# A two-layer hybrid decoder trunk on one core: GpSimd's tables and weight sums go to VectorE, the squared relu goes to ScalarE

## The chip, the core and the metric

The kernel runs on one core of a Trainium2 chip. The metric is the time of one execution on the device in microseconds (us); less is better. The engines are named as in the profile: PE is TensorE's matmul stream (PEld its weight loads), DVE is VectorE, ACT is ScalarE, POOL is GpSimd, and SP is SyncE, whose queue issues all the DMAs of this kernel. Each engine works through its own queue of instructions in order.

## What is computed

Two layers over a sequence of 1,024 positions and 1,024 channels, in float32. The reference, cut down:

```python
for l in range(2):
    h = rms_norm(x, mix_norm_g[l])
    # one projection: stick-breaking q/k/v, sliding-window q/k/v, two gates
    sb_q, sb_k, sb_v, sw_q, sw_k, sw_v, gate_logits = split(h @ w_in[l])
    y_sb = stick_breaking_attention(sb_q, sb_k, sb_v) @ w_branch_sb[l]
    q = apply_rope(rms_norm(sw_q, q_norm_g[l]), cos, sin)
    k = apply_rope(rms_norm(sw_k, k_norm_g[l]), cos, sin)
    y_swa = sliding_window_sink_attention(q, k, sw_v, sinks[l]) @ w_branch_swa[l]
    g = sigmoid(gate_logits).reshape(B, S, 2, D)
    x = x + (g[:, :, 0] * y_sb + g[:, :, 1] * y_swa) @ w_out[l]
    h2 = rms_norm(x, mlp_norm_g[l])
    x = x + square(relu(h2 @ w_up[l])) @ w_down[l]      # 1024 -> 4096 -> 1024
```

## The kernel before

Every product is made in three matmuls: each operand is split into a high part in the type fp32r (a cast on ScalarE) and the rest (a subtraction on VectorE), and the function `three` multiplies high by high, high by rest and rest by high. So a 128-row block of an operand costs one ScalarE instruction and one VectorE instruction (`split`, lines 1266 and 1269; `fetch`, lines 332 and 335, for other weights) before TensorE can use it.

A layer runs in four stages: norm and gates, sliding-window attention beside stick-breaking attention, merge and output projection, and the MLP. The MLP's two products are each made by a scheme with seven block products in the place of eight (numbered "1" to "7"), whose operands are sums and differences of quarters of the matrices.

- **First product** (`up_phase`). The weights of one of 16 pairs come in two DMAs of 512 KB, `ra` and `rb`, into two buffers named `raw`. Products 1 and 2 use the halves of `ra` as they are. Products 3 to 7 use sums: `operands` makes four of them from `a11`, `a12` (`ra`) and `a21`, `a22` (`rb`), in place or into a `stage` buffer, and then splits them into buffers `wh` and `wl`. The four sums are GpSimd's (line 1283, the "G" branch of `two`). TensorE does the products of a pair in the order 1, 2, 6, 5, 3, 4, 7, and each product is 12 matmuls of 512 columns. `pair` adds the seven results into four blocks on VectorE (line 1583), squares their positive part (`relu2`, line 1542), makes the sums for the second product (line 1280) and writes all of it to a scratch tensor `u_scr`. A buffer of `rb` comes free when product 7's operand has been split.
- **Second product** (`down_phase`). SP loads 512 KB pieces of `u_scr` and of `w_down` into buffers named `dr`, and they are split into tiles named `operand`.
- **Sliding-window attention.** `consts` scales a table `gt` and the sinks `snk`; `tables` multiplies `gt` with the rotation of one block of 128 positions into a table `tab`, eight per layer, and saves it. Those three are GpSimd's too (lines 510, 512, 547). An iteration's VectorE chain reads `tab` (lines 626 and 628), adds (633), splits (662, 644), and TensorE transposes the result (lines 668 and 650).

The order of the instructions on each engine is set when the program is built: a planner (`Plan`) gives every step an engine and a cost, such as

```python
yield "G", gps(n)        # n * .00195 + .4 us on GpSimd
yield "D", dve(n)        # n * .00104 + .068 us on VectorE
yield "A", act(n)        # n * .00083 + .095 us on ScalarE
```

and writes the instructions out in the order in which its own clock comes to them. That order is then fixed, so an instruction whose input is late holds up all that stands behind it on its engine.

Of the kernel before, what the change touches and what calls it, by code (L numbers as in the profile page):

```python
# [12 lines left out]
AF = mybir.ActivationFunctionType  # L13
ALU = mybir.AluOpType
AX = mybir.AxisListType

P = 128
T = 1024
D = 1024
HD = 64  # L20
# [178 lines left out]
def tile_hybrid_trunk(ctx: ExitStack, tc: tile.TileContext, x, g_mix, g_mlp, g_rope, sinks, rope,  # L199
                      w_swa, w_qk, w_v, w_gate, w_br, w_out, w_up, w_down, out):  # L200
    nc = tc.nc
# [50 lines left out]
    def act(n):  # L252
        return n * .00083 + .095

    def dve(n):
        return n * .00104 + .068

    def gps(n):
        return n * .00195 + .4
# [7 lines left out]
    def moved(n):  # L267

        return "M", n / 380e3, 0
# [24 lines left out]
    def stage_tile():  # L294
        return gp.tile([P, 512], F32, tag="stage", name="stage", bufs=4)
# [184 lines left out]
    def swa_phase(l, base, sw, swp, hT, normed, o_scr, tab_scr, finished, tail, projected):  # L480
# [13 lines left out]
        cev = [Event(plan) for _ in range(2)]  # L494

        def consts(g):
            if g:
                yield wevs[1][0]
            gt = None
            if g == 0:  # L500
                yield "S", .45
                gt = sw.tile([P, 2, 5, HD], F32, name="gt")
                nc.sync.dma_start(out=gt, in_=g_rope[l].broadcast_to([P, 2 * 5 * HD]).rearrange("p (a b c) -> p a b c", a=2, b=5))
            yield "S", .45
            snk = sw.tile([P, 2, 4], F32, tag="snk", name="snk", bufs=2)
            nc.sync.dma_start(out=snk[:, 0], in_=sinks[l, g].broadcast_to([P, 4]))
            yield moved(640 * 512)
            if g == 0:
                yield "G", gps(512)
                nc.gpsimd.tensor_scalar(gt[:, :, 0:4], gt[:, :, 0:4], -0.125, None, ALU.mult)  # L510
            yield "G", .1
            nc.gpsimd.tensor_scalar(snk[:, 1], snk[:, 0], -1.0, None, ALU.mult)
            cev[g].set((gt, snk))

        for g in range(2):
            plan.spawn(consts(g), base + 590 + g)
# [14 lines left out]
        def tables(g, t):  # L531
            yield cev[g]
            if g:
                yield kept[t]
            yield tab_s
            yield "S", .45
            tab = sw.tile([P, 2, 5, HD], F32, tag="tab", name="tab", bufs=3)
            if g:
                nc.sync.dma_start(out=tab, in_=tab_scr[t].rearrange("p (a b c) -> p a b c", a=2, b=5))
                yield moved(640 * 512)  # L540
                tabs[g][t].set((tab, tab_s.release))
                return
            rt = sw.tile([P, 2, HD], F32, tag="rt", name="rt", bufs=2)
            nc.sync.dma_start(out=rt, in_=rope[t])
            yield moved(128 * 512)
            yield "G", gps(640)
            nc.gpsimd.tensor_tensor(tab, cev[g].value[0], rt.unsqueeze(2).broadcast_to([P, 2, 5, HD]), ALU.mult)
            use = Shared(2, tab_s.release)
            tabs[g][t].set((tab, use.done))
            yield "S", .45, base + 1900  # L550
            nc.sync.dma_start(out=tab_scr[t].rearrange("p (a b c) -> p a b c", a=2, b=5), in_=tab)
            kept[t].set()
            yield moved(640 * 512)
            use.done()
# [247 lines left out]
        for g in range(2):  # L802
            for t in range(NT):
                plan.spawn(tables(g, t), base + 1000 + (g * NT + t) * 10)
                plan.spawn(iteration(g, t), base + 1000 + (g * NT + t) * 10)
# [457 lines left out]
    def split(op, j, src, n, lo_eng="D", ev=True):  # L1263

        yield "A", act(n)
        nc.scalar.copy(op.hi(j, n), src)  # L1266
        if lo_eng == "D":
            yield "D", dve(n)
            nc.vector.tensor_tensor(op.lo(j, n), src, f32(op.hi(j, n)), ALU.subtract)  # L1269
        else:  # L1270
            yield "G", gps(n)
            nc.gpsimd.tensor_tensor(op.lo(j, n), src, f32(op.hi(j, n)), ALU.subtract)
        if ev:
            for i in range(n // 512):
                op.ready[j + i].set()

    def two(eng, out, a, b, op, n=512):
        if eng == "D":
            yield "D", dve(n)
            nc.vector.tensor_tensor(out, a, b, op)  # L1280
        else:
            yield "G", gps(n)
            nc.gpsimd.tensor_tensor(out, a, b, op)  # L1283
# [125 lines left out]
    def up_phase(l, base, quads, normed, small, u_scr, u_ev, fetched, tail_raw, tail_ring, multiplied, finished):  # L1409
# [11 lines left out]
        def weights(evs):  # L1421
            yield fetched
            for p in range(PRE):
                got = yield from fetch_raw(p)
                plan.spawn(early(got, evs[p]), base + 75000 + FIRST + p)
            for p in range(16):
                c, i = divmod(p, 4)
                rs = []
                for f in (8 * c + i, 8 * c + 4 + i):
                    got = yield from fetch_raw(f)  # L1430
                    rs.append(got)
                if p == 15:
                    tail_raw.set()
                done = Event(plan)
                plan.spawn(operands(rs, evs[p], done, p), base + 80000 + p * 100 - (BOOST if p < 3 else 0))
                yield done

        def firsts(ra, ea, evs):
            yield ring
            o1, o2 = pair_of()  # L1440
            yield ea
            yield from split(o1, 0, ra[:, :512], 512)
            evs["1"].set(o1)
            yield from split(o2, 0, ra[:, 512:], 512)
            evs["2"].set(o2)
# [9 lines left out]
        def pair_of():  # L1455
            t = [wp.tile([P, 1024], F32R, tag=tag, name=tag, bufs=4) for tag in ("wh", "wl")]
            use = [2]

            def free():
                use[0] -= 1  # L1460
                if use[0] == 0:
                    ring.release()

            def view(tile_, o):
                return lambda j, n=512: tile_[:, o:o + n]

            return [Operand(view(x_, 0), view(x_, 512), 1, free) for x_ in t]

        def operands(rs, evs, done, p):
            (ra, ea), (rb, eb) = rs  # L1470
            a11, a12, a21, a22 = ra[:, :512], ra[:, 512:], rb[:, :512], rb[:, 512:]
            if p >= PRE:
                yield from firsts(ra, ea, evs)
            else:
                yield ea
            yield eb
            yield stages
            s1 = stage_tile()
            yield from two("G", s1, a21, a22, ALU.add)
            yield from two("G", a21, a11, a21, ALU.subtract)  # L1480
            yield from two("G", a11, s1, a11, ALU.subtract)
            e4 = Event(plan)

            def fourth():
                yield from two("G", a12, a12, a11, ALU.subtract)
                e4.set()

            plan.spawn(fourth(), plan.cur.rank + 1)
            yield ring
            o6, o5 = pair_of()  # L1490
            yield from split(o6, 0, a11, 512)
            evs["6"].set(o6)
            yield from split(o5, 0, s1, 512)
            stages.release()
            evs["5"].set(o5)
            yield ring
            o3, o4 = pair_of()
            yield e4
            yield from split(o3, 0, a12, 512)
            evs["3"].set(o3)  # L1500
            raws.release()
            done.set()
            yield from split(o4, 0, a22, 512)
            evs["4"].set(o4)
            yield ring
            if p == 15:
                tail_ring.set()
            o7, other = pair_of()
            other.done()
            yield from split(o7, 0, a21, 512)  # L1510
            raws.release()
            evs["7"].set(o7)
# [21 lines left out]
        def pair(p, evs):  # L1534
# [3 lines left out]
            yield flight  # L1538

            def relu2(t):  # L1540
                yield "D", dve(512)
                nc.vector.scalar_tensor_tensor(t, t, 0.0, t, ALU.max, ALU.mult)

            def keep(n, t, then=None):

# [47 lines left out]
            def second(pm, b):  # L1593
                yield e["p1"]
                yield small
                yield small.value[1]
                t = fresh()
                yield from add(t, pm, e["p1"].value)
                b.free()
                e["c11"].set()  # L1600
                yield from relu2(t)
                e["a11"].set(t)
                plan.spawn(keep("1", t, e["kept11"].set), rank - 49)
# [498 lines left out]
```

## Time and profile before

| | before |
|---|---|
| median of three runs | 2775.42 us (2772.57 to 2777.33) |
| profiled execution, its own time | 2772.42 us |
| its span in the trace | 2770.6 us |
| PE busy | 2708.4 us, 98% |
| DVE busy | 1920.9 us, 69% |
| ACT busy | 1246.6 us, 45% |
| POOL busy | 221.1 us, 8% |

The span runs from the first to the last instruction that the profiler saw; the execution's own time is 1.8 us more. Matmuls overlap in the records, so TensorE's busy time is not all work at its full speed; how many matmuls stand in a stretch tells more.

### The profile page before, as it was taken

The numbers are of one execution on the slowest core, as the hardware profiler recorded it, in microseconds if no ns is written. First come the engines' busy times: TensorE is split into PE (matmuls) and PEld (weight loads), VectorE is DVE, ScalarE is ACT, GpSimd is POOL, SyncE is SP. The second block draws the span as 40 slices with busy tenths as digits, with TensorE's granted clock in tenths as the row PEclk, the third lists the DMA queues.
The fourth block names the chain that finished last, engine by engine and source line by source line (L and its number), as shares of the span: only waits on it lengthen the run. The fifth ranks groups of instructions, "written<-read, shape, count | busy, mean of one in ns | idle before, by whom it ended". The sixth has DMA issues, their size and how long they took to land. (4 is left out here: it accounts for less than half of the span.)

```text
span 2770.6 us, 37073 instructions
## 1 busy us (share of the span) xinstructions
PE 2708.4 (98%) x13568; PEld 2281.4 (82%) x13568; DVE 1920.9 (69%) x3247; ACT 1246.6 (45%) x2521; POOL 221.1 (8%) x233
## 2 busy tenths in 40 slices
PE   7999999999989999999999999999999999999999
PEld 6888888888868877888888888888887777778887
DVE  6665888765587677767666658887547867678664
ACT  5776566642432223333457765565425222234332
POOL 1000000000032221000010000000000322200000
PEclk9999999999999999999999999999999999999999
DMA  5232222264124347996333222123530445389972
GB/s 171 81 92 62 61 62 58 68 225 157 31 103 167 132 161 270 354 370 244 137 116 99 71 62 65 50 64 126 180 135 32 144 127 166 126 314 354 342 265 92
DMA packets 159382, 411.00 MB, mean 148 GB/s; under 512 B 18656, under 2 KB 32992, under 8 KB 159200
## 3 DMA queue, kind: packets, MB, share of 16 engines
q1 hardware_dynamic: 159200, 408.63, 42.9%
q8 instruction: 107, 1.75, 0.3%
q14 instruction: 75, 0.61, 0.1%
HBM read 285.88 MB, written 114.29 MB: 144 GB/s over the span
## 5 line engine op out<-in xcount | busy, mean ns | idle before, releaser
L1266 ACT CAST operand<-dr 128x1024 fp32r<-128x1024 f32 x224 | 220.1, 1049 | 369.7 <-PE bank L348 173.7
L346 PE MATMUL bank<-operand 128*128 128x512 f32 x896 | 350.3, 391 | 5.8 <-ACT operand L1266 5.8
L347 PE MATMUL bank<-operand 128*128 128x512 f32 x896 | 350.5, 391 | 3.0 <-DVE operand L1269 3.0
L348 PE MATMUL bank<-operand 128*128 128x512 f32 x896 | 349.7, 390 | 0.0
L1269 DVE TENSOR_TENSOR operand<-dr,operand 128x1024 fp32r<-128x1024 f32 x224 | 262.7, 1218 | 121.0 <-ACT operand L1266 117.9
L346 PE MATMUL bank<-hT,wh 128*128 128x512 f32 (+1 forms) x776 | 312.4, 403 | 0.0
L348 PE MATMUL bank<-hT,wl 128*128 128x512 f32 (+1 forms) x776 | 302.9, 390 | 0.0
L347 PE MATMUL bank<-hT,wh 128*128 128x512 f32 (+1 forms) x776 | 302.2, 389 | 0.0
L1266 ACT CAST wh<-raw 128x512 fp32r<-128x512 f32 x128 | 79.4, 621 | 442.2 <-POOL raw L1283 254.7
L1269 DVE TENSOR_TENSOR wh<-raw,wh 128x512 fp32r<-128x512 f32 x128 | 102.5, 801 | 146.7 <-ACT wh L1266 146.7
L346 PEld LDWEIGHTS bank<-operand 128*128 128x128 f32 x896 | 168.8, 188 | 42.8 <-ACT operand L1266 7.5
L347 PEld LDWEIGHTS bank<-operand 128*128 128x128 f32 x896 | 168.9, 189 | 39.0 <-DVE operand L1269 4.3
L348 PEld LDWEIGHTS bank<-operand 128*128 128x128 f32 x896 | 169.0, 189 | 35.0
L348 PEld LDWEIGHTS bank<-hT,wl 128*128 128x128 f32 x776 | 146.3, 189 | 31.6
L347 PEld LDWEIGHTS bank<-hT,wh 128*128 128x128 f32 x776 | 147.1, 190 | 23.3
L346 PEld LDWEIGHTS bank<-hT,wh 128*128 128x128 f32 x776 | 147.3, 190 | 22.9
L335 DVE TENSOR_TENSOR wl<-raw,wh 128x1024 fp32r<-128x1024 f32 x88 | 107.0, 1219 | 57.5 <-ACT wh L332 56.8
L332 ACT CAST wh<-raw 128x1024 fp32r<-128x1024 f32 x88 | 92.2, 1050 | 106.6 <-PE bank L348 76.6
L1283 POOL TENSOR_TENSOR stage<-raw 128x512 f32<-128x512 f32 x32 | 53.0, 1657 | 863.1 <-ACT kept L1376 437.9
L999 DVE TENSOR_TENSOR_SCAN keep<-keep 128x128 f32<-128x128 f32 (+3 forms) x128 | 100.0, 808 | 16.2 <-ACT keep L988 16.2
L1058 DVE TENSOR_TENSOR tl<-bank,th 128x512 fp32r<-128x512 f32 (+1 forms) x160 | 97.6, 626 | 17.9 <-ACT th L1056 16.2
L988 ACT ACTIVATE keep<-bank 128x128 f32<-128x128 f32 (+1 forms) x192 | 91.3, 499 | 38.9 <-PE bank L982 23.4
(199 smaller groups left out, 6676.0 us busy)
## 6 DMA issues: line engine op xcount, KB each, us to landing
dr<-in_w_down_dram SPq DMA_DIRECT2D x144, 512.0 KB, 8.1
dr<-u_scr SPq DMA_DIRECT2D x112, 512.0 KB, 7.5
u_scr<-up SPq DMA_DIRECT2D x160, 256.0 KB, 4.4
raw<-in_w_up_dram SPq DMA_DIRECT2D x68, 512.0 KB, 4.3
raw<-in_w_gate_dram SPq DMA_DIRECT2D x32, 512.0 KB, 4.2
g_scr<-stage SPq DMA_DIRECT2D x64, 256.0 KB, 2.4
gate<-g_scr SPq DMA_DIRECT2D x64, 256.0 KB, 3.0
u_scr<-stage SPq DMA_DIRECT2D x64, 256.0 KB, 3.7
```

The lines of the kernel that those rows point to most:

```text
L332: nc.scalar.copy(hi[:, :n], raw[:, :n])
L335: nc.vector.tensor_tensor(lo[:, :n], raw[:, :n], f32(hi[:, :n]), ALU.subtract)
L346: nc.tensor.matmul(ps_ap, ah, bh, start=first, stop=False)
L347: nc.tensor.matmul(ps_ap, ah, bl, start=False, stop=False)
L348: nc.tensor.matmul(ps_ap, al, bh, start=False, stop=last)
L988: nc.scalar.activation(keep[:, lo:512], z, AF.Sigmoid, scale=-1.0)
L999: nc.vector.tensor_tensor_scan(later[:, ::-1], later[:, ::-1], later[:, ::-1], ini, ALU.mult, ALU.bypass)
L1058: nc.vector.tensor_tensor(tl[:, :n], tr[:, :n], f32(th[:, :n]), ALU.subtract)
L1266: nc.scalar.copy(op.hi(j, n), src)
L1269: nc.vector.tensor_tensor(op.lo(j, n), src, f32(op.hi(j, n)), ALU.subtract)
L1283: nc.gpsimd.tensor_tensor(out, a, b, op)
```

## The change

The rotation tables, the scaling of `gt` and of the sinks, and the four sums of each pair's weights are given to VectorE. The squared relu, one VectorE instruction per block, becomes a Relu and a Square on ScalarE, in place. What stays on GpSimd are masks at the start and single-column fills.

```diff
             if g == 0:
-                yield "G", gps(512)
-                nc.gpsimd.tensor_scalar(gt[:, :, 0:4], gt[:, :, 0:4], -0.125, None, ALU.mult)
-            yield "G", .1
-            nc.gpsimd.tensor_scalar(snk[:, 1], snk[:, 0], -1.0, None, ALU.mult)
+                yield "D", dve(512)
+                nc.vector.tensor_scalar(gt[:, :, 0:4], gt[:, :, 0:4], -0.125, None, ALU.mult)
+            yield "D", .12
+            nc.vector.tensor_scalar(snk[:, 1], snk[:, 0], -1.0, None, ALU.mult)
...
-            yield "G", gps(640)
-            nc.gpsimd.tensor_tensor(tab, cev[g].value[0], rt.unsqueeze(2).broadcast_to([P, 2, 5, HD]), ALU.mult)
+            yield "D", dve(640)
+            nc.vector.tensor_tensor(tab, cev[g].value[0], rt.unsqueeze(2).broadcast_to([P, 2, 5, HD]), ALU.mult)
...
-            yield from two("G", s1, a21, a22, ALU.add)
-            yield from two("G", a21, a11, a21, ALU.subtract)
-            yield from two("G", a11, s1, a11, ALU.subtract)
+            yield from two("D", s1, a21, a22, ALU.add)
+            yield from two("D", a21, a11, a21, ALU.subtract)
+            yield from two("D", a11, s1, a11, ALU.subtract)
...
-                yield from two("G", a12, a12, a11, ALU.subtract)
+                yield from two("D", a12, a12, a11, ALU.subtract)
...
             def relu2(t):
-                yield "D", dve(512)
-                nc.vector.scalar_tensor_tensor(t, t, 0.0, t, ALU.max, ALU.mult)
+                yield "A", 2 * act(512)
+                nc.scalar.activation(t, t, AF.Relu)
+                nc.scalar.activation(t, t, AF.Square)
```

Since the planner's costs change with the engine, it writes the instructions out in another order. In the changed kernel the lines after `relu2` are one further on (1584 for 1583).

On VectorE, where the MLP of the first layer begins. Before, from the norm's last scalar ahead of the eighth norm's product (line 425) on:

```order
L365 TENSOR_TENSOR y_7974<-y_7974,rs_a_8002 128x1
L425 SCALAR_TENSOR_TENSOR h_7970<-xt7_7276,y_7974,g_7317 128x1024
L1356 TENSOR_TENSOR t2_7283<-stage_8021,t2_7283 128x4x128
L1280 TENSOR_TENSOR kept_7285<-kept_7285,stage_8021 128x4x128
L1280 TENSOR_TENSOR kept_7284<-stage_8021,kept_7284 128x4x128
L1280 TENSOR_TENSOR kept_7286<-kept_7286,kept_7284 128x4x128
L1583 TENSOR_TENSOR up_8072<-bank_7983,stage_7987 128x512
```

Now, with the first pair's four sums (those that write `stage_8009` and `raw`) in between:

```order
L365 TENSOR_TENSOR y_7974<-y_7974,rs_a_8002 128x1
L1280 TENSOR_TENSOR stage_8009<-raw_7980 128x512
L425 SCALAR_TENSOR_TENSOR h_7970<-xt7_7276,y_7974,g_7317 128x1024
L1356 TENSOR_TENSOR t2_7283<-stage_8021,t2_7283 128x4x128
L1280 TENSOR_TENSOR raw_7980<-raw_7949,raw_7980 128x512
L1280 TENSOR_TENSOR kept_7285<-kept_7285,stage_8021 128x4x128
L1280 TENSOR_TENSOR raw_7949<-stage_8009,raw_7949 128x512
L1280 TENSOR_TENSOR kept_7286<-kept_7286,kept_7284 128x4x128
L1280 TENSOR_TENSOR raw_7949<-raw_7949 128x512
L1269 TENSOR_TENSOR wh_8072<-raw_7949,wh_8072 128x512
```

The sums now share VectorE's queue with the norm and the quarters' cuts; the split of product 6's operand (`wh_8072`) follows on the fourth sum.

On VectorE again, in the second layer's steady state, around the operands of the last pair. Before: the additions of the fourth and the seventh product of the pair before it (`bank_22651`, `bank_22669`), and between them the split of the last pair's operand 6 (`wh_22681`), made from GpSimd's sums:

```order
L1583 TENSOR_TENSOR up_22650<-bank_22632,up_22631 128x512
L1542 SCALAR_TENSOR_TENSOR up_22650<-up_22650 128x512
L1583 TENSOR_TENSOR stage_22564<-bank_22651,stage_22564 128x512
L1269 TENSOR_TENSOR wh_22681<-raw_22579,wh_22681 128x512
L1583 TENSOR_TENSOR stage_22564<-bank_22669,stage_22564 128x512
L1583 TENSOR_TENSOR up_22631<-bank_22669,up_22631 128x512
L1269 TENSOR_TENSOR wl_22682<-stage_22655,wl_22682 128x512
```

Now: the same pair's additions of products 6, 5, 3 and 4 (`bank_22714`, `bank_22738`, `bank_22760`, `bank_22781`), with the last pair's four sums and the split of its operand 6 (`wh_22772`) among them:

```order
L1584 TENSOR_TENSOR stage_22694<-bank_22714,stage_22694 128x512
L1269 TENSOR_TENSOR wl_22712<-raw_22661,wl_22712 128x512
L1280 TENSOR_TENSOR stage_22753<-raw_22683 128x512
L1280 TENSOR_TENSOR raw_22683<-raw_22661,raw_22683 128x512
L1584 TENSOR_TENSOR up_22759<-bank_22738,stage_22694 128x512
L1280 TENSOR_TENSOR raw_22661<-stage_22753,raw_22661 128x512
L1280 TENSOR_TENSOR raw_22661<-raw_22661 128x512
L1269 TENSOR_TENSOR wh_22772<-raw_22661,wh_22772 128x512
L1584 TENSOR_TENSOR up_22780<-bank_22760,up_22759 128x512
L1269 TENSOR_TENSOR wl_22773<-stage_22753,wl_22773 128x512
L1584 TENSOR_TENSOR stage_22694<-bank_22781,stage_22694 128x512
```

Operand 6 of the next pair stood behind the addition of product 4, and stands now behind that of product 5, two products earlier.

On SP, where the second layer's first product hands over to its second. Before, from the write of the last pair but one's block (`stage_22564`) on:

```order
L1547 DMA u_scr1_19671<-stage_22564 128x512
L1547 DMA u_scr1_19671<-up_22631 128x512
L1756 DMA dr_22730<-u_scr1_19671 128x1024
L1547 DMA u_scr1_19671<-up_22722 128x512
L1547 DMA u_scr1_19671<-up_22650 128x512
L1547 DMA u_scr1_19671<-up_22586 128x512
L1547 DMA u_scr1_19671<-up_22738 128x512
L1547 DMA u_scr1_19671<-stage_22564 128x512
L1770 DMA dr_22772<-in_w_down_dram 128x1024
L1756 DMA dr_22782<-u_scr1_19671 128x1024
```

Now, from the same place on, two loads of `u_scr` stand ahead of that write, and the first load of `w_down` among the writes:

```order
L1757 DMA dr_22815<-u_scr1_19735 128x1024
L1757 DMA dr_22837<-u_scr1_19735 128x1024
L1548 DMA u_scr1_19735<-stage_22694 128x512
L1548 DMA u_scr1_19735<-up_22759 128x512
L1757 DMA dr_22873<-u_scr1_19735 128x1024
L1548 DMA u_scr1_19735<-up_22863 128x512
L1771 DMA dr_22882<-in_w_down_dram 128x1024
L1548 DMA u_scr1_19735<-up_22780 128x512
```

The second piece of `u_scr` and the first of `w_down`, both wanted by the first `operand` tiles, have moved up by several writes.

## Rows read from the trace of the kernel before

**Rows 1.** Page, part 1: busy us and share of the span, instructions, per engine.

```profile
PE 2708.4 (98%) x13568; PEld 2281.4 (82%) x13568; DVE 1920.9 (69%) x3247; ACT 1246.6 (45%) x2521; POOL 221.1 (8%) x233
```

**Rows 2.** Windows: stretch, length, then PE, PEld, DVE, ACT, POOL; PEclk, DMA, GB/s.

```profile
910.00:980.00 70.00, 70.00 (x311) 57.95 (x310) 51.95 (x82) 14.44 (x26) 15.80 (x13) 1.00 0.48 166
788.00:797.00 9.00, 5.12 (x14) 3.83 (x15) 5.64 (x9) 2.80 (x5) 3.81 (x3) 0.81 0.00 0
2160.00:2169.00 9.00, 5.37 (x15) 3.99 (x16) 5.88 (x9) 2.80 (x5) 3.60 (x3) 0.81 0.01 4
980.00:1050.00 70.00, 68.71 (x299) 55.45 (x298) 49.03 (x77) 16.57 (x30) 20.30 (x16) 1.00 0.41 133
2240.00:2450.00 210.00, 204.97 (x888) 165.02 (x887) 149.93 (x235) 47.57 (x86) 53.36 (x42) 1.00 0.46 145
1076.00:1092.00 16.00, 11.39 (x40) 8.18 (x40) 12.21 (x14) 8.07 (x8) 0.00 (x0) 0.89 1.02 389
2454.00:2470.00 16.00, 11.75 (x43) 8.49 (x42) 12.22 (x15) 8.08 (x8) 0.00 (x0) 0.89 1.02 407
```

**Rows 3.** Timeline, first MLP's start: start us, us, instruction, [idle before <-releaser].

```profile
760.11 1.60 DVE L1280 TENSOR_TENSOR stage<-kept 128x512 f32<-128x512 f32 x1
761.63 1.25 DVE L365 TENSOR_TENSOR y<-y,rs_a 128x1 f32<-128x1 f32 x1
762.92 2.37 DVE L425 SCALAR_TENSOR_TENSOR h<-xt,y,g 128x1024 f32<-128x1024 f32 x1
765.21 1.75 DVE L1356 TENSOR_TENSOR t<-stage,t 128x512 fp32r<-128x512 f32 x1
...
784.34 2.48 DVE L1269 TENSOR_TENSOR taken<-up,taken 128x512 fp32r<-128x512 f32 x4
...
781.44 6.53 POOL L1283 TENSOR_TENSOR stage<-raw 128x512 f32<-128x512 f32 x1 [15.03 <-DVE up L1583]
...
790.68 0.62 ACT L1266 CAST wh<-raw 128x512 fp32r<-128x512 f32 x1 [7.57 <-POOL raw L1283]
...
791.35 0.50 PE L346 MATMUL bank<-t,wh 128*128 128x512 f32 x1 [3.51 <-ACT wh L1266]
```

**Rows 4.** Timeline, one pair of the second layer's first product, around 2440 us.

```profile
2435.71 1.29 POOL L1283 TENSOR_TENSOR stage<-raw 128x512 f32<-128x512 f32 x1 [14.50 <-DMA raw<-in_w_up_dram]
...
2439.77 0.62 ACT L1266 CAST wh<-raw 128x512 fp32r<-128x512 f32 x1 [8.57 <-POOL raw L1283]
...
2440.42 1.24 DVE L1269 TENSOR_TENSOR wh<-raw,wh 128x512 fp32r<-128x512 f32 x1 [5.80 <-ACT wh L1266]
...
2440.78 0.40 PE L347 MATMUL bank<-t,wh 128*128 128x512 f32 x1
2441.72 0.50 PE L348 MATMUL bank<-t,wh 128*128 128x512 f32 x1 [0.54 <-DVE wh L1269]
```

**Rows 5.** Groups by form: count, busy us, mean ns; last, page part 6: KB, us to landing.

```profile
L1283 POOL TENSOR_TENSOR raw<-raw 128x512 f32<-128x512 f32 x64 | 86.2, 1347 | 5.0
L1542 DVE SCALAR_TENSOR_TENSOR up<-up 128x512 f32<-128x512 f32 x96 | 68.5, 714 | 1.0
L1403 ACT COPY up<-kept 128x512 f32<-128x512 f32 x8 | 4.6, 618 | 1.6 <-DVE kept L1280 1.6
...
raw<-in_w_up_dram SPq DMA_DIRECT2D x68, 512.0 KB, 4.3
```

**Rows 6.** Timeline, second layer's hand-over to the second product, two engines.

```profile
2456.23 1.04 ACT L1266 CAST operand<-dr 128x1024 fp32r<-128x1024 f32 x1 [5.09 <-DMA dr<-in_w_down_dram]
...
2457.33 0.50 PE L346 MATMUL bank<-operand 128*128 128x512 f32 x1 [2.17 <-ACT operand L1266]
```

**Rows 7.** Timeline, first layer's sliding-window start, VectorE and TensorE.

```profile
59.56 1.83 DVE L633 TENSOR_TENSOR m<-m,m 128x320 f32<-128x320 f32 x1
...
71.83 0.48 DVE L633 TENSOR_TENSOR m<-m,m 128x320 f32<-128x320 f32 x1
...
62.43 0.72 PE L668 MATMUL bank<-ident_r,st 128*128 128x128 f32 x4 [5.04 <-DVE st L662]
```

## The prediction

> **What bounds the kernel now.** First the page: TensorE is busy for 98% of the span [rows 1], so the most that any edit can win is what TensorE waits, and the matmuls that run slowly after a wait. Then the windows, to see how much that is and where. A stretch without a wait holds 311 matmuls in 70 us [rows 2], 0.225 us each; where a stretch holds fewer, the missing ones times 0.225 us is what it lost, waits and slow matmuls together. (Some records can be missing from a trace, so where many are counted I take a value between this loss and the idle time.) By that the MLPs lose: at the first layer's start, 788 to 797 us, 9.0 - 14 x 0.225 = 5.85 us, and at the second's 9.0 - 15 x 0.225 = 5.6; in the first product's steady state 12 matmuls or 2.7 us (idle 1.3) in the first layer, and 45 matmuls or 10.1 us (idle 5.0) in the second; at the hand-over to the second product 16 - 40 x 0.225 = 7.0 and 16 - 43 x 0.225 = 6.3 us [rows 2]. The granted clock of the two starts is 0.81, of the hand-overs 0.89, and 1.00 elsewhere: after a wait TensorE runs for a while at the lower of its two levels, 1.2 GHz in the place of 2.4. Last the timelines, to see who is late there.
>
> **The start of an MLP: GpSimd and VectorE hold each other up.** At 781.44 us GpSimd begins a sum that takes 1.3 us elsewhere, and it takes 6.53 [rows 3, 4]; it ends when VectorE's run of splits ends (four of `taken` at 784.34, 2.48 us together, so 0.60 from start to start). ScalarE's cast for product 6 waits 7.57 us for GpSimd, and TensorE waits 3.51 us for that cast [rows 3]. The other way round, while GpSimd makes the first four sums, four VectorE instructions take 1.60, 1.25, 2.37 and 1.75 us [rows 3]. From the first one's start to the last one's end are 6.85 us; at the free pace (0.60 for 512 columns, 1.20 for 1024, under 0.1 for the single column) they need 2.5, so VectorE loses 4.3.
>
> After the change VectorE has in this stretch, up to the last split of `taken`, eight sums and three splits of pair operands more and two squared relus fewer: +9 x 0.60 = 5.4 us, less the 4.3 that it no longer loses, so that split comes 1.1 us later, at about 788 for 786.8. Product 7 ends that much later, but product 6's operand has been split before it (the order places it among the eight sums), so TensorE goes on at once. It gains 5.85 - 1.1 = 4.75 us, in the second layer 4.5. I take 9.2 for both. Bounds: 2 (the added work reaches TensorE fully, 3 us more per layer) and 16 (product 7 isn't late and the waits ahead of it shrink too).
>
> **The first product's steady state.** The second layer's pairs wait each time in the same way: the DMA of `rb` lands at 2435.7, GpSimd makes four sums of 1.3 us, ScalarE's cast waits for the third of them, VectorE's split takes 1.24 us beside the fourth instead of 0.60, and TensorE waits 0.54 us within product 6; its matmuls start 0.94 apart there [rows 4]. Even the 0.6 us of the slow split would cover that wait. The four sums cost VectorE 4 x 0.60 = 2.4 us per pair in the place of 5.4 on GpSimd, and the relus that leave it give back 4 x 0.60, so its load stays (16 pairs x 2 layers x 4 of each kind; the count of line 1542 in rows 5 is for one of its tiles, the other tile has the remaining 32). More than that: the sums now stand behind product 6 of the pair before, two products or 2 x 12 x 0.225 = 5.4 us earlier in the queue. What is late next? The sums wait for `rb`, whose buffer comes free when the last operand 7 has been split, at about the end of the last product 7. From there to product 6's end are three products, 8.1 us; such a load lands 4.3 us after its issue [rows 5], so some 3.8 us are to spare. I take 8 us for the second layer and 2 for the first, between idle time and missing matmuls. Bounds 0 and 12.8.
>
> **The relu on ScalarE** costs up to 2 x 0.62 = 1.24 us by the nearest row, a copy of the same shape between the same memories, in the place of 0.71 on VectorE [rows 5]. ScalarE gets 256 passes, about 158 us, and is busy for 45% now, 14 us of 70 in this stage [rows 1, 2]; what covers it is that most of the stage's ScalarE time is idle. The later block matters to the sums for the second product and to their write to `u_scr`, which are read tens of microseconds later; only the last pair's are close, at the hand-over. There the row that bears on it is 2456.23: the second cast of an `operand` waited 5.09 us for a load of `w_down` [rows 6]. In the changed ScalarE queue two such casts stand ahead of the last pair's block 1. By the SP order both read `u_scr` pieces that are now loaded earlier, so I count nothing. Without that cover the block is 10 us late; it is wanted only after three steps of 48 matmuls, 32 us.
>
> The Trainium skill speaks against this edit: "ScalarE: Activation LUTs", rules for kernel authors, says that relu and the like belong on VectorE. The rows agree with it on the price of one block. If TensorE waited for each of the 128 blocks, as the rule would have it, this term would be 128 x 0.53 = 68 us of loss in the place of 0; that is the second slower rival below.
>
> **The hand-over.** TensorE waits 2.17 us for a cast that waits for `w_down` [rows 6], and the DMA share is 1.02 [rows 2]. The changed queue loads two pieces of `u_scr` and the first of `w_down` several writes earlier, because the additions of product 7 no longer stand behind a late split. That spreads the loads, but DMA stays near its limit, so I take half of 7.0 + 6.3, 6.6 us. Bounds -5 and 13.3: a relu of two passes and two casts ahead of the write cost 2.5 us per layer if they count.
>
> **The tables.** VectorE gets 16 tables, by columns 0.60 x 640 / 512 = 0.75 us each, two scalings of `gt` of about 0.6 (bounds 0.3 and 0.7: half a 512-column sum and a whole one) and four tiny ones: 13 us. Most fall into VectorE's gaps. At the stage's start TensorE waits 5.04 us for a chain in which line 633 takes 1.83 us beside GpSimd and 0.48 later [rows 7]: 1.35 us, in both layers 2.7. I take 2.7. Bounds: -8 (ten tables in the chain, 0.75 us each) and +10 (the whole wait in both layers).
>
> **Sum.** 9.2 + 10 + 6.6 + 2.7 = 28.5 us. The profiled execution took 2772.4 us; the median is 3.0 above it. 2772.4 - 28.5 + 3.0 = 2746.9, so 2747 us, 1.0% faster.
>
> **Rivals.** 0.2% of the time, 5.5 us, is about what a measurement of this kernel can tell from no change.
> - *Half of it.* The hand-over stays as it is, since DMA is full there, and the start of the MLP gains only its lower bound: 2 + 10 + 2.7 = 14.7, so 2761 us. For it: a DMA share of 1.02; against it: the loads move. Chance 0.22.
> - *No change.* VectorE's queue takes over the role of GpSimd: the sums wait in it for `rb`, all that follows waits with them, and TensorE waits as now: 2772 to 2778 us. For it: VectorE is the engine most others wait for; against it: 3.8 us to spare at `rb`, and 30% of VectorE idle [rows 1]. 0.07.
> - *Slower by the tables.* The planner writes out the sliding-window stage in another order; ten tables stand ahead of the chain that TensorE waits for, 7.5 us, and each wait costs about half as much again at the lower clock: 11 us. It decides if the MLP gains less than 5 us: 2781 us. 0.04.
> - *Slower by the relu.* Two passes in the way of the casts: 128 blocks at 0.53 us more are 68 us if TensorE waited for each; with the gains 2772 - 28 + 68 + 3 = 2815 us. It decides from half of the blocks on. Against it: ScalarE idles 55 us of 70 there [rows 2], so a cast can be made up elsewhere. 0.03.
>
> My forecast has the rest, 0.64, and its own range is 2736 to 2757. The two gaining cases hold 0.86 and reach from 2734 to 2766, with the bounds of the starts and the hand-overs in it; the range is 2733 to 2767. Faster 0.86, same 0.07, slower 0.07.
>
> **What would show it.** Right: product 6's first matmul follows on product 7 at the MLP's start, at a clock of 1.00; 309 to 311 matmuls per 70 us in both layers' first product; the four sums at 0.6 us each; the hand-overs lose 2 to 5 us. Wrong: a VectorE sum waiting for the DMA of `raw` for several microseconds with TensorE waiting behind it, or more idle time of TensorE in the sliding-window stage than the waits of now.

## The result, and the profile after

The changed kernel takes 2726.84 us (median of four runs, 2726.55 to 2727.98) against 2776.33 for the kernel before (2772.57 to 2777.33; a fourth run stands beside the three of the table above): ratio 0.9825, 95% interval 0.9808 to 0.9842. That is 49.5 us less, faster as forecast, but by more than the 28.5 us of the sum, and 2726.84 lies below the range of 2733 to 2767. Between the two profiled executions the gain is 44.6 us (2772.57 to 2727.98); the other 4.9 us are their places among the runs, the lowest of before and the highest of after.

The page, part 1, after (its row of before is [rows 1]): TensorE lost 17 us of its busy time and GpSimd nearly all; ScalarE got 156 us more.

```profile
PE 2691.2 (99%) x13568; PEld 2280.9 (84%) x13568; DVE 1904.0 (70%) x3269; ACT 1402.4 (51%) x2777; POOL 8.9 (0%) x83
```

Windows of after, at the places of [rows 2], in the same columns: the first product in both layers, the starts of both MLPs, both hand-overs.

```profile
910.00:980.00 70.00, 70.00 (x311) 57.96 (x310) 49.94 (x80) 35.91 (x62) 0.00 (x0) 1.00 0.44 151
2170.00:2400.00 230.00, 230.00 (x1017) 190.44 (x1016) 169.44 (x267) 113.77 (x195) 0.00 (x0) 1.00 0.46 153
763.00:772.00 9.00, 2.44 (x7) 1.38 (x6) 9.00 (x16) 6.26 (x12) 0.00 (x0) 0.70 0.16 58
2114.00:2123.00 9.00, 2.44 (x7) 1.38 (x6) 9.00 (x16) 6.26 (x12) 0.00 (x0) 0.74 0.16 58
1064.00:1080.00 16.00, 15.67 (x69) 12.61 (x68) 10.59 (x13) 9.46 (x12) 0.00 (x0) 1.00 1.03 407
2412.00:2428.00 16.00, 15.80 (x70) 12.77 (x69) 11.47 (x13) 9.08 (x12) 0.00 (x0) 1.00 1.03 410
```

The second layer's first product has no wait left: 1017 matmuls in 230 us are 0.226 us each. The hand-overs hold 69 and 70 matmuls in 16 us instead of 40 and 43, at the same DMA share as before. But 763 to 772 us is new: TensorE does 7 matmuls there, at a granted clock of 0.70, while VectorE is busy for all of the 9 us. The view of what TensorE waited for, after, over the whole program (us in total, times, longest):

```profile
PE bank L346 <- ACT t L1354: 12.4, 2, 6.2
PE bank L436 <- DVE rs_a L359: 10.8, 1, 10.8
PE bank L436 <- DVE h L425: 3.2, 4, 2.0
PE bank L668 <- DVE st L662: 2.1, 1, 2.1
```

The second row is the kernel's own start. The first is the new wait, once per layer, and the timeline of after shows whose it is:

```profile
757.73 0.69 DVE L1280 TENSOR_TENSOR stage<-raw 128x512 f32<-128x512 f32 x1
...
766.75 0.69 DVE L1269 TENSOR_TENSOR wh<-raw,wh 128x512 fp32r<-128x512 f32 x1
767.35 0.69 DVE L1280 TENSOR_TENSOR kept<-stage,kept 128x512 f32<-128x512 f32 x1
767.95 0.69 DVE L1269 TENSOR_TENSOR quarter<-kept,quarter 128x512 fp32r<-128x512 f32 x1
768.56 0.69 DVE L1280 TENSOR_TENSOR stage<-kept 128x512 f32<-128x512 f32 x1
...
769.28 0.62 ACT L1354 CAST t<-stage 128x512 fp32r<-128x512 f32 x1 [1.16 <-DVE stage L1280]
...
769.95 0.80 PE L346 MATMUL bank<-t,wh 128*128 128x512 f32 x1 [6.20 <-ACT t L1354]
771.11 0.80 PE L347 MATMUL bank<-t,wh 128*128 128x512 f32 x1 [0.36 <-DVE t L1356]
```

`t2`, the quarters' side of product 6, is made on VectorE too. Its last part stands behind the first pair's four sums and the splits that follow on them, and TensorE, which has nothing else to do, waits 6.20 us for it. TensorE's wait of [rows 3] for GpSimd's sums is gone in return.

To see where the 44.6 us came from I added up, in each trace, what stands between the starts of successive matmuls beyond their usual 0.228 us (gaps over 0.245 us only), by the kernel's parts. "First product" is its steady state and the hand-over. Each line is one profiled execution; in the kernels whose first product still loses time, that part differs by a few us between executions.

| us that TensorE lost | attention | MLP starts | first product |
|---|---|---|---|
| before | 40.0 | 27.3 | 25.3 |
| after | 28.6 | 20.2 | 1.1 |
| sums_alone | 39.8 | 21.2 | 0.7 |
| relu_alone | 40.9 | 23.1 | 24.4 |
| tables_alone | 31.3 | 28.4 | 30.5 |
| without_tables | 38.3 | 20.2 | 0.2 |
| sums_vector_old_order | 40.0 | 17.8 | 3.0 |
| sums_gpsimd_new_order | 29.9 | 25.5 | 0.3 |
| tables_gpsimd_new_order | 34.5 | 20.4 | 0.0 |
| operands_first | 39.7 | 28.1 | 0.7 |
| mixing_first | 28.7 | 19.4 | 0.2 |
| mixing_then_taken | 29.9 | 23.7 | 1.0 |
| extra_sums_after | 29.4 | 29.0 | 30.8 |

So the gain is 11.4 us in the attention, 7.1 at the MLP starts, 24.2 in the first product and its hand-over. Of the last, counted by the same gaps, the steady state gains 11.3 and the hand-over 12.9.

### The profile page after: what moved, and what is told of

The parts are those of the page before. It is cut to its first block, busy times and chain, and to the rows that moved or that the text cites. A ratio compares the mean times of both kernels' runs of the same rounds, so it can differ in the third digit from the quotient of the medians.

```text
span 2726.2 us, 37142 instructions
## 1 busy us (share of the span) xinstructions
PE 2691.2 (99%) x13568; PEld 2280.9 (84%) x13568; DVE 1904.0 (70%) x3269; ACT 1402.4 (51%) x2777; POOL 8.9 (0%) x83
## 4 chain that ended last, share of the span: by engine, by line
PE 95%; DVE 2%; ACT 1%; DMA 1%; issue 0%; SPq 0%; DVEq 0%; ACTq 0%
PE bank L346 28%; PE bank L347 28%; PE bank L348 27%; PE bank L1050 2%; PE bank L1083 1%; PE bank L979 1%; PE bank L980 1%; PE bank L1082 1%; PE bank L694 1%; PE bank L436 1%; PE bank L761 1%; PE bank L784 0%; PE bank L783 0%; PE bank L668 0%; PE bank L982 0%
## 5 line engine op out<-in xcount | busy, mean ns | idle before, releaser
L347 PEld LDWEIGHTS bank<-hT,wh 128*128 128x128 f32 x776 | 147.2, 190 | 23.7 <-DVE hT L395 0.2
L988 ACT ACTIVATE keep<-bank 128x128 f32<-128x128 f32 (+1 forms) x192 | 91.3, 499 | 38.7 <-PE bank L982 23.1
L1058 DVE TENSOR_TENSOR tl<-bank,th 128x512 fp32r<-128x512 f32 (+1 forms) x160 | 97.5, 626 | 18.2 <-ACT th L1056 16.6
L1056 ACT CAST th<-bank 128x512 fp32r<-128x512 f32 (+1 forms) x160 | 83.3, 546 | 49.2 <-PE bank L1050 46.1
L1280 DVE TENSOR_TENSOR dr<-dr 128x1024 f32<-128x1024 f32 x64 | 78.1, 1224 | 40.7 <-DMA dr<-t_scr 16.2
```

Source lines behind the costliest of these rows:

```text
L347: nc.tensor.matmul(ps_ap, ah, bl, start=False, stop=False)
L988: nc.scalar.activation(keep[:, lo:512], z, AF.Sigmoid, scale=-1.0)
L1056: nc.scalar.copy(th[:, :n], tr[:, :n])
L1058: nc.vector.tensor_tensor(tl[:, :n], tr[:, :n], f32(th[:, :n]), ALU.subtract)
```

## The experiments

**Which part of the change?** Four kernels, each with some hunks of the change's diff and the rest as before.

```diff
sums_alone:       two("G", ...) -> two("D", ...), four times
relu_alone:       relu2 as Relu and Square on ScalarE
tables_alone:     gt, snk and tab on VectorE
without_tables:   sums_alone and relu_alone together
```

> Only the four weight sums move to VectorE; tables stay on GpSimd, the squared relu on VectorE. Theory A (contention: VectorE and GpSimd hold each other up, and the sums are the cause in the MLP): the MLPs come out as in the changed kernel and the attention as before, -42.7 + 11.5 = some 31 us less than before, 2745 us; steady state 311 matmuls in 70 us, hand-overs without the 5 us wait. Theory B (load: the sums help only because the relus leave VectorE's queue): VectorE has 64 x 4 x ... more than before in each pair, 4 x 0.60 = 2.4 us, so the hand-over and the steady state keep their waits, 10 to 15 us less than before, about 2763 us.

> Only the squared relu moves to ScalarE as two passes. Theory A (contention): GpSimd still makes the sums, so 2774 to 2780 us, no gain, and at the hand-over the 5 us wait stays. Theory B (load on VectorE): with 4 x 0.71 us less on VectorE in each pair the split behind the sums comes earlier, and the steady state of the second layer and the hand-over gain 10 to 20 us, about 2760 us.

> Only the rotation tables and the scalings move to VectorE. Theory A (contention): the sliding-window stages gain what the changed kernel gained there, 11 us, about 2765 us, with the first wait of TensorE at line 668 falling from 5.04 to about 2.1 us. Theory B (the gain there comes from the other parts of the change, by the order): under 3 us, about 2774 us.

> Sums on VectorE and relu on ScalarE, tables on GpSimd: the changed kernel without its tables. Theory A (contention, stage by stage): 31 to 33 us less than before, 2744 us, its attention stages as before. Theory B (parts act together through the order): as fast as the changed kernel, 2727 us, or as sums alone plus relu alone.

Measured, as medians and as ratios to the kernel before: the sums alone 2739.3 us (0.9864, 0.9850 to 0.9877), the relu alone 2769.3 (0.9971, 0.9960 to 0.9982), the tables alone 2764.3 (0.9959, 0.9946 to 0.9972), sums and relu 2737.9 (0.9858, 0.9843 to 0.9874). The sums give 36.7 us, the tables 11.7, and the two add up to nearly the whole. The relu gives 6.7 us alone, which neither theory had (none by A, 10 to 20 by B). By its trace they come from the MLP starts (23.1 us lost instead of 27.3), and the first product, where B looked for them, loses 24.4 instead of 25.3: theory B of the load fell. On top of the sums the relu gives 1.4 us, which can't be told from nothing.

**The engine, or the order that the planner writes?** The edits let the planner count a step at one engine's cost and give it to the other. `two` gets a branch for it, which the four sums alone use (cut down; only the first of them is shown).

```diff
 # sums_vector_old_order (on before)
+        elif eng == "GD":
+            yield "G", gps(n)
+            nc.vector.tensor_tensor(out, a, b, op)
...
-            yield from two("G", s1, a21, a22, ALU.add)
+            yield from two("GD", s1, a21, a22, ALU.add)
 # sums_gpsimd_new_order (on after; tables_gpsimd_new_order does it at lines 510, 512, 547)
+        elif eng == "DG":
+            yield "D", dve(n)
+            nc.gpsimd.tensor_tensor(out, a, b, op)
...
-            yield from two("D", s1, a21, a22, ALU.add)
+            yield from two("DG", s1, a21, a22, ALU.add)
```

> Before, with the four sums made by VectorE but planned at GpSimd's costs, so that all else keeps the order of before. If the engine makes the gain (GpSimd's sums take 1.3 us and more and slow VectorE down): most of the 36.7 us that the sums alone gave, under 2750 us. If the new order makes it (operands split two products earlier, loads moved at the hand-over): 10 us or less, over 2765 us, with the hand-overs' waits still there.

> The changed kernel, with the four sums made by GpSimd but planned at VectorE's costs, so that all else keeps the new order. If the engine makes the gain: 25 us or more are lost against the changed kernel's 2727 us, 2752 us or more, with VectorE instructions of 1.2 to 2.4 us beside the sums and TensorE waiting for ScalarE's casts that wait for GpSimd. If the order makes it: at most 10 us are lost, 2737 us or less.

> The changed kernel, with the tables and scalings made by GpSimd but planned at VectorE's costs. If GpSimd's work beside VectorE's chain costs the 11 us in the sliding-window stages: 2735 to 2738 us, with line 633 at 1.8 us again at the first wait of TensorE. If the order of the stage does: 2729 us or less, and the wait at line 668 stays at 2.1 us.

Measured: VectorE in the old order 2740.2 us (0.9872, 0.9858 to 0.9887), GpSimd in the new order 2731.9 (0.9840, 0.9824 to 0.9857). Apart from who makes the sums, the instructions stand on every engine in the order of before in the first kernel, and in that of after in the second. Both theories are right by their own test and wrong by the other's. The engine alone brings 33.8 us, and the order brings all but 5.1 us of the change with the sums still on GpSimd, where they are as slow as ever. The groups by form of that kernel, 2180 to 2400 us:

```profile
L1269 DVE TENSOR_TENSOR wh<-raw,wh 128x512 fp32r<-128x512 f32 x47 | 53.4, 1137 | 3.4 <-ACT wh L1266 3.3
L1283 POOL TENSOR_TENSOR raw<-stage,raw 128x512 f32<-128x512 f32 x12 | 19.3, 1609 | 7.1 <-DVE wh L1269 6.9
```

A split takes 1137 ns on the mean and the third sum 1609, and yet this stage loses nothing. So instructions that slow each other down, the prediction's reason for the steady state, do not by themselves make TensorE wait. In the tables both count: with GpSimd making them in the new order it is 2735.0 us (0.9853, 0.9838 to 0.9868), 8.1 more than after, as expected if GpSimd's work costs the time. By the traces 34.5 us are lost in the attention, about halfway between 28.6 and 40.0. The first wait at line 668 is long again, 4.48 us (2.08 after), but not by line 633, which takes 0.48 us. This time it is line 614, an instruction on five columns ahead of it in VectorE's queue, that is slow beside GpSimd's table:

```profile
59.23 1.88 POOL L547 TENSOR_TENSOR tab<-gt,rt 128x640 f32<-128x640 f32 x1 [6.95 <-DMA rt<-in_rope_dram]
...
59.64 1.50 DVE L614 SCALAR_TENSOR_TENSOR a<-v,a 128x5 f32<-128x5 f32 x1
...
62.78 0.51 PE L668 MATMUL bank<-ident_r,st 128*128 128x128 f32 x4 [4.48 <-DVE st L662]
```

**The loop.** What do the engine and the order have in common? The timeline of before, one pair from its product 6 to the next:

```profile
2340.66 1.24 DVE L1269 TENSOR_TENSOR wh<-raw,wh 128x512 fp32r<-128x512 f32 x1 [5.86 <-ACT wh L1266]
...
2350.36 0.68 DVE L1269 TENSOR_TENSOR wh<-raw,wh 128x512 fp32r<-128x512 f32 x1
...
2351.07 0.33 SPq L1416 DMA_DIRECT2D raw<-in_w_up_dram  x1
...
2355.50 1.29 POOL L1283 TENSOR_TENSOR stage<-raw 128x512 f32<-128x512 f32 x1 [14.14 <-DMA raw<-in_w_up_dram]
...
2358.24 1.29 POOL L1283 TENSOR_TENSOR raw<-stage,raw 128x512 f32<-128x512 f32 x1
...
2359.56 0.62 ACT L1266 CAST wh<-raw 128x512 fp32r<-128x512 f32 x1 [8.29 <-POOL raw L1283]
...
2360.21 1.24 DVE L1269 TENSOR_TENSOR wh<-raw,wh 128x512 fp32r<-128x512 f32 x1 [5.44 <-ACT wh L1266]
...
2360.66 0.39 PE L346 MATMUL bank<-t,wh 128*128 128x512 f32 x1
```

VectorE stands still for 5.86 us, since the next instruction in its queue is the split of operand 6, which waits for the sums. Then it works off what has piled up; operand 7's split comes 9.7 us later (2350.36). That frees the buffer of `rb`, whose load is issued at once (2351.07), lands at 2355.50, is summed, cast, and split again at 2360.21: 19.55 us for this turn. From pair 6 to pair 15 the first sums start at 2256.47 and 2435.71, 19.9 us a turn, where the 84 matmuls of a pair need 19.04. The lead of the sums, from the end of the third to product 6's first matmul, falls until it is used up, and from then on the loop sets the pace. (The split of operand 6, 1.24 us beside GpSimd instead of 0.68, is part of the turn: what the two engines cost each other counts there.) Pairs of the second layer, numbered from 0 (worked out from the timelines):

| lead, us | pair 4 | pair 8 | pair 12 | pair 15 |
|---|---|---|---|---|
| before | 1.6 | 1.3 | 0.7 | 0.8 |
| relu_alone | 4.1 | 3.4 | 0.7 | 0.7 |
| sums_vector_old_order | 4.3 | 6.7 | 6.7 | 6.7 |
| sums_gpsimd_new_order | 10.8 | 13.3 | 13.5 | 13.6 |
| after | 11.9 | 11.9 | 11.9 | 11.9 |
| operands_first | 3.3 | 10.9 | 11.8 | 11.8 |
| extra_sums_after | 5.2 | 1.5 | 0.8 | 0.8 |

Faster sums shorten the loop, and so does an earlier split of operand 7; either takes it under 19.04, and then the lead grows to a level at which it stays, 11.9 us in the changed kernel. (What sets that level, the number of buffers perhaps, was not tested.) To show it without either part of the change, one number of the kernel before:

```diff
-  plan.spawn(operands(rs, evs[p], done, p), base + 80000 + p * 100 - (BOOST if p < 3 else 0))
+  plan.spawn(operands(rs, evs[p], done, p), base + 80000 + p * 100 - (BOOST if p < 3 else 150))
```

> Before, with one number changed: the operands of pairs 3 to 15 rank 150 earlier, so that the split of operand 7, which frees the buffer of rb, stands ahead of one or two additions on VectorE. GpSimd still makes the sums. Theory of the loop (split of operand 7, load of rb, four sums, cast and split of operand 6, product 6, and back; before it takes 19.4 to 19.9 us, TensorE's pair 19.04): the loop falls under 19.04 us, the sums are ready several us ahead of product 6, and the steady state and the hand-over gain together 10 to 24 us, 2752 to 2766 us. Theory of contention beside product 6 (each pair waits 0.5 us for a split slowed by the fourth sum): the split is still slow, no gain at the hand-over, 2770 us or more.

Measured: 2748.3 us (0.9899, 0.9884 to 0.9914), 27.6 less than before, with GpSimd's sums and the old tables and relu (the rank moves rows on ScalarE and SP too, none on TensorE). Its timeline for pair 12 (the one of before is pair 11), and its windows:

```profile
2344.54 0.33 SPq L1416 DMA_DIRECT2D raw<-in_w_up_dram  x1
...
2349.12 1.73 POOL L1283 TENSOR_TENSOR stage<-raw 128x512 f32<-128x512 f32 x1 [12.62 <-DVE wh L1269]
...
2365.70 0.39 PE L346 MATMUL bank<-t,wh 128*128 128x512 f32 x1
```

```profile
2290.00:2360.00 70.00, 70.00 (x310) 57.99 (x309) 52.43 (x80) 15.89 (x28) 22.97 (x16) 1.00 0.46 152
1070.00:1086.00 16.00, 16.00 (x72) 13.15 (x71) 12.82 (x16) 5.83 (x6) 0.00 (x0) 1.00 1.03 406
2426.00:2442.00 16.00, 15.58 (x69) 12.57 (x68) 12.83 (x17) 7.50 (x8) 0.00 (x0) 1.00 1.02 385
```

The load of `rb` is issued 21.2 us ahead of product 6 instead of 9.6, GpSimd's first sum waits for VectorE here rather than for the DMA, and the hand-overs lose nothing either: 72 and 69 matmuls in 16 us. The gain goes past the 24 us expected at most. Then the loop was made longer, with the plan left as it is:

```diff
             yield from two("D", s1, a21, a22, ALU.add)
+            for _ in range(4):                            # extra_sums_after
+                nc.vector.tensor_tensor(s1, a21, a22, ALU.add)
             yield from two("G", s1, a21, a22, ALU.add)
+            for _ in range(2):                            # extra_sums_before
+                nc.gpsimd.tensor_tensor(s1, a21, a22, ALU.add)
```

> The changed kernel, with the first sum of each pair made five times over, the plan left as it is: 4 x 0.60 = 2.4 us more on VectorE in each of the 32 pairs. Theory of the loop: the sums are made 11.9 us ahead of product 6 and lose 2.4 of that, so the steady state keeps 311 matmuls in 70 us; only the first pairs, where VectorE's queue is the bound, lose 2 to 4 us per layer: 2730 to 2736 us. If instead VectorE's load bounds the stage: 2.4 us x 32 pairs = 77 us more, towards 2800 us.

> Before, with the first sum of each pair made three times over by GpSimd, the plan left as it is: 2 x 1.37 = 2.7 us more in each of the 32 pairs. Theory of the loop: it rises from 19.4 to 19.9 us to 22 or more, and nearly every pair of both layers takes that: 50 to 80 us more, 2825 to 2855 us. If the loop has slack, or the sums are off the path for most pairs: under 30 us more.

Measured: on before 2862.5 us (1.0311, 1.0294 to 1.0329), 86.7 us more for 32 x 2.7 = 86.4 us of GpSimd's time, a little over what the loop was expected to cost. From pair 2 to pair 15 a turn takes 22.0 us on the mean in the first layer and 22.5 in the second, 19.2 and 19.7 in before, and 79.7 of the 86.7 us lie in the turns from pair 0 to pair 15: nearly every pair pays in full. On after 2769.4 us (0.9972, 0.9961 to 0.9983), 42.5 more than after, neither of the two times expected. Windows of extra_sums_after:

```profile
910.00:980.00 70.00, 70.00 (x311) 57.96 (x310) 58.51 (x93) 32.63 (x57) 0.00 (x0) 1.00 0.49 165
2360.00:2430.00 70.00, 68.47 (x296) 54.78 (x295) 57.01 (x90) 31.28 (x55) 0.00 (x0) 1.00 0.50 160
2443.00:2459.00 16.00, 8.44 (x29) 5.48 (x27) 11.32 (x14) 8.06 (x10) 0.00 (x0) 0.82 0.99 341
```

From pair 2 to pair 11 of the first layer TensorE runs at full pace, but the lead falls pair by pair, in the second layer by 0.3 to 1.2 us (table), until it is gone. Then waits and a bad hand-over return (29 matmuls in the last window). The first product loses 30.8 us, 22.7 of them at the hand-overs, and the MLP starts 8.8 more than after. VectorE is busy for 57 to 59 us of 70 there, so it isn't its load alone. My mistake was to set the 2.9 us that the four extra sums take (the fifth starts 2.90 after the first) against the lead of 11.9 us. A lead is a stock, used up over the 16 pairs of a layer; what counts is by how much the loop stays under 19.04 us in each pair, and in the changed kernel that is less than 2.9.

**The new wait at the MLP's start.** Two tries to take it away:

```diff
 # mixing_first (on after); mixing_then_taken has this too
-BOOST = 5100
+BOOST = 900
 # mixing_then_taken, in operands, ahead of the first sum
+            if p == 1:
+                for e in quads.ops["7"].ready:
+                    yield e
```

> The changed kernel with BOOST 900 for 5100: the steps of the first three pairs' operands rank behind the sums of the quarters, so the last part of t2 (line 1356) stands some ten instructions earlier on VectorE. If the new wait of 6.2 us at each MLP's start is VectorE's queue ahead of t2: both waits fall to under 2 us, and with the matmuls at the lower clock behind them 12 to 14 us are gained on the changed kernel, 2713 to 2715 us. If it only moves on to the next operand of the pair (5 or 3, whose split now comes later): 2723 to 2730 us.

> The changed kernel with BOOST 900 as in the last series, and the sums of pair 1 held back until operand 7 of the quarters (the last taken) has been split. If the wait for taken of 2.4 us in the last series came from the sum that waited 2.02 us for the DMA of raw ahead of it in VectorE's queue: that wait goes, 3 to 8 us less than the changed kernel, 2719 to 2724 us. If the wait then goes to the operands of pair 1, which come later: 2726 to 2732 us.

Measured: 2728.0 us (0.9828, 0.9813 to 0.9843) and 2732.2 (0.9843, 0.9828 to 0.9857), against 2726.8 of after. What TensorE waited for in mixing_first, 750 to 800 us:

```profile
PE bank L347 <- DVE taken L1269: 2.6, 2, 2.4
PE bank L346 <- ACT t L1354: 1.4, 1, 1.4
PE bank L347 <- DVE t L1356: 0.7, 1, 0.7
```

The wait for `t2` falls from 6.2 to 1.4 us, and 2.4 us for `taken` appear further on. With those split first, the wait moves to operand 6 of pair 1, for which TensorE waits 3.87 us. Each time what is put first is early and the next thing late. Neither of the two kernels beats the changed one. (VectorE's sums in the old order lose less at the starts, 17.8 us instead of 20.2; that order was not tried together with the rest of the change.)

## Why the prediction was wrong

The direction and the places were right, and the sizes were not. The measured median is 20 us below the forecast. The hand-over was taken 6.3 us too small, the tables 8.7 and the steady state 1.3, the MLP starts 2.1 too large; the offset of the median makes some 4, and 1.9 lie outside the gaps that I counted.

- **The first product's steady state and the hand-over**: 10 + 6.6 = 16.6 us in the sum, 24.2 measured (11.3 + 12.9). Two steps failed. In "What is late next?" I took each pair by itself: a wait of 0.54 us within product 6, from a split slowed by the fourth sum, and afterwards 3.8 us to spare at `rb`, since operand 7 would be split at about the end of the last product 7. The wait was the loop's, and a pair that gains hands its lead to the next one: in the changed kernel a load of `rb` is issued at 2304.51, 17.5 us ahead of the last product 7's end and 22.9 ahead of the product 6 that it feeds (2327.42):

```profile
2304.51 0.33 SPq L1416 DMA_DIRECT2D raw<-in_w_up_dram  x1
...
2327.42 0.39 PE L346 MATMUL bank<-t,wh 128*128 128x512 f32 x1
```

  For the steady state that made little difference, since nearly all of it was counted. The other step is the half that I took of the hand-over, "DMA stays near its limit". It does stay there (1.03), and the hand-overs lose next to nothing, because what they need is an earlier start and not less traffic. In before, SP's queue stands 12.8 us at the write of a block that VectorE finishes only after the late split of operand 6 ([rows 4], 2440.42), and the first load of `w_down` stands behind it. The SP queue of before, then of after:

```profile
2444.09 0.32 SPq L1547 DMA_DIRECT2D u_scr<-stage  x1
...
2449.44 0.63 SPq L1770 DMA_DIRECT2D dr<-in_w_down_dram  x1
```

```profile
2404.24 0.38 SPq L1771 DMA_DIRECT2D dr<-in_w_down_dram  x1
```

  So this load is issued 12.7 us ahead of the last `taken` matmul instead of 5.3 (2404.24 to 2416.95, and before 2449.44 to 2454.77). That is the lead's doing and not that of SP's new order, on which I had put it. sums_vector_old_order keeps SP's order of before, issues that load 10.2 us ahead (2416.81 to 2427.00), and loses 3.0 us in the whole of the first product; extra_sums_after keeps the new order, has no lead left, issues it 4.3 us ahead (2443.18 to 2447.49), and loses 22.7 us at the hand-overs.
- **The MLP starts**: 9.2 us in the sum, 7.1 measured. Product 6 of the second pair does follow on product 7 without a wait. I had followed the pair's side of product 6 and not the quarters' side, `t2`, which the added sums push back. The prediction's bound for added work reaching TensorE in full was in the right place. The last two experiments did not avoid it: VectorE has no gap over 0.3 us from 751 to 774 us in the changed kernel.
- **The tables**: 2.7 us in the sum, 11.4 by the traces and 11.7 by the medians of tables_alone (8.7 in its attention stages by its own trace), a little above the upper bound of 10. The step that failed: I had priced one instruction, line 633, at one wait and doubled it. In the second layer it was another: a VectorE instruction on five columns, which takes 0.16 us elsewhere. Timeline of before, then of after:

```profile
1428.10 1.53 POOL L547 TENSOR_TENSOR tab<-gt,rt 128x640 f32<-128x640 f32 x1 [6.68 <-DVE vt L596]
...
1428.41 1.24 DVE L614 SCALAR_TENSOR_TENSOR a<-v,a 128x5 f32<-128x5 f32 x1 [0.32 <-ACT a L612]
...
1431.09 0.72 PE L668 MATMUL bank<-ident_r,st 128*128 128x128 f32 x4 [3.35 <-DVE st L662]
```

```profile
1409.46 0.16 DVE L614 SCALAR_TENSOR_TENSOR a<-v,a 128x5 f32<-128x5 f32 x1
```

  In before it ends with GpSimd's table, at 1429.6, and TensorE waits 3.35 us for the chain that it stands in; after the change that wait is gone. The Trainium skill, "SBUF — State Buffer", in "SBUF: two separate sides", says that the two engines share a pair of ports as an exclusive lock, which the instruction that starts first keeps to its end, where VectorE's instruction has two inputs in SBUF; the trace agrees for this one, which ends within 0.02 us of the table. So even five columns can cost VectorE over a microsecond beside GpSimd. How the rest of the gain, the order's, comes about in this stage was not taken apart.
- **The relu**: 0 in the sum, and 1.4 us of gain on top of the sums, within the noise. Its two passes take 632 and 634 ns by the groups of after, as priced. The rule of the Trainium skill weighed there ("ScalarE: Activation LUTs", Rules for kernel authors) holds for the price of one block, but the loss did not come: ScalarE is busy for 51% of the span, and none of TensorE's waits of after is for one of the passes.
- **The offset**: 3.0 us were added for the median's place above the profiled execution. After the change it lies 1.1 us below, so that term was the place of one execution among the runs and no property of the kernel.

Of the rivals, "half of it" failed at the hand-over, and the three others found nothing in the trace. The gain of 49.5 is 42.7 us of gaps, 1.9 of other time between the profiled executions, and 4.9 of their places among the runs.

## What to carry to other kernels

Where a buffer comes free only after the work that its load feeds, follow the whole loop once and compare it with the time that the busiest engine needs for a turn: if it is longer, even by 0.5 us, every turn pays once the lead is used up, and any edit that shortens it enough, by engine, order or rank, wins about the same time (the first product's loss fell from 25.3 us to 3.0, 0.3 and 0.7 here), so their gains don't add. Look at how the lead changes from turn to turn, not at how large it is, and carry it on to the next stage, whose first loads it moves. Where an engine has no gap, as VectorE at the MLP's start, the two new orders tried here only chose who waits.

## What the runs showed of the hardware

Beside GpSimd's sums, in sums_gpsimd_new_order, a split took up to 1.78 us and a sum up to 1.85, for 0.68 and 1.29 alone, and with a lead of 10.8 us and more that cost TensorE nothing in the steady state. A VectorE instruction on five columns took 1.24 us (before) and 1.50 us (tables_gpsimd_new_order) beside GpSimd's table, for 0.16 alone.

The four runs of the changed kernel lie within 1.4 us, while eleven of the kernel before spread over 6.9 (2774.87 to 2781.75). That the loop, whose every turn waits for a DMA, makes this spread is not shown: four runs of extra_sums_before, where nearly every pair waits in the loop, lie within 2.3 us (2861.15 to 2863.40).
